# Copies, joins and weight roundings of the block products, tied to the program's order on ScalarE and VectorE

## The chip, the core and the metric

The kernel runs on one core of a Trainium2 chip. A core has a matrix engine (TensorE, "PE" in the profile, with its weight loads as "PEld"), VectorE ("DVE"), ScalarE ("ACT"), GpSimd ("POOL") and a queue that issues transfers ("SP"). Each engine works through its own list of instructions in the order in which the list was written; engines wait for each other by semaphores. The metric is the device time of one execution in microseconds.

## The reference

One inference step of a two-layer network over 640 tokens (512 latent, 128 context). Layer 0 mixes tokens with a state-space scan, layer 1 with differential attention. After each mixer comes the same kind of feed-forward network, and that is where the change lies:

```python
def conv_ffn(h, up_w, conv_w, conv_b, down_w):
    u = dwconv(h @ up_w, conv_w, conv_b)
    a, v = jnp.split(u, 2, axis=-1)
    return (jax.nn.silu(a) * v) @ down_w
```

Here `h` is 640 x 1024, `up_w` is 1024 x 5632, the convolution runs over three neighbouring tokens, and `down_w` is 2816 x 1024.

## The kernel before

Everything is kept transposed: 128 channels lie on the 128 partitions, the 640 tokens along the free axis. Every dense product is made of three matmuls: each operand is split into a rounded high part and the remainder, and high x high, high x low and low x high are added. For the weights the split is done on the chip. `cast` (L257) takes a loaded weight tile `raw` of 128 x 1024, rounds it on ScalarE into `whi` and subtracts on VectorE to get `wlo`; both go through `split_w` (L268). `nextw` (L277) hands out the next weight unit and has the one a few places further on cast; in the part of interest that is three units ahead (`AHEAD`). There are five buffers for cast units.

The 2816 hidden channels are 22 "pairs" of 128 (one half for `a`, one for `v`). The first `STD` of them (16 in layer 0, 5 in layer 1) are computed directly. The others, 6 in layer 0 and 17 in layer 1, are computed by the class `Blocks` (L46): a pair costs seven half-size products instead of eight, at the price of sums of the results. A product (L113) is 12 matmuls of 128 x 320. In `pair` (L138) product 1 goes into the PSUM area `a`, ScalarE copies it into the first half of `ua`; product 2 goes into `b` and VectorE adds ("joins") it to that; product 6 accumulates on `a`, and ScalarE copies again; product 5 goes into `c`; product 7 accumulates on `a`, ScalarE copies it into `uv` and VectorE joins `c`. Two products of a pair are finished inside the next pair: `third` (L159, product 3 on `c`, a join) and `fourth` (L164, product 4 on `a`, a copy), after which `epilogue` follows: a convolution of `ua` and one of `uv` (each one ScalarE instruction and four on VectorE), SiLU on ScalarE, a multiplication on VectorE, and the split of the result into `mh` (ScalarE) and `ml` (VectorE).

The program's order of the seven products in a pair is therefore 1, 2, 3 (of the pair before), 6, 4 (of the pair before, with its epilogue), 5, 7. Each weight unit serves two consecutive products, so a unit is cast at every other one.

The three areas lie in PSUM tiles of two halves each, columns 0 to 511 and 512 to 1023, three tiles in rotation (`banks`, L129). In every second pair ("even" below, the first of a stage among them) `a` and `b` are the halves of one tile, `ba` in the trace, and `c` is the first half of the next, `bb`. In the pair after it ("odd") `a` is the second half of that `bb`, and `b` and `c` are the halves of `bc`. The pairs run in stages with the down-projection (`po`) between them: 6 pairs in layer 0, then 3, 7 and 7 in layer 1. The two late products of a stage's last pair run after the first down-projection tile (`between`).

What sets the order: the program is written as one sequence, and a scheduler at compile time places each engine's instructions in an order of its own, as early as buffers and data allow by its estimate. Only an instruction passed through `tc.keep_in_program_order` is tied: it must stand behind the instruction that was written before it for the same engine. The helpers `act`, `tt`, `stt` and `mm` (L218 to L231) do this only while `fixed` is set, which is so in the kernel's first microseconds and not in the feed-forward networks. All ScalarE instructions of the helper show as line L222 in the profile, VectorE's as L225 and L228, the matmuls as L231; the tile names tell them apart.

## Time and profile before

| what | us |
|---|---|
| median of three runs (1838.42 to 1843.67) | 1839.06 |
| the profiled execution | 1841.66 |
| its span, first to last instruction | 1839.9 |
| first and last stretch with block products: layer 0 | 899 to 981 |
| layer 1, three stages | 1451 to 1496, 1540 to 1635, 1679 to 1775 |

The mean granted clock of TensorE was 0.995. Times inside the execution are counted from the span's start. In the chain that ended last, a piece such as "PE ba x12" is a run of twelve matmuls into that tile. A matmul's own duration in the trace overlaps its neighbours', so the length of a run is read from such pieces: twelve matmuls without a gap take 1.76.

### The profile page before, as it was taken

The numbers are of one execution on the slowest core, as the hardware profiler recorded it, in microseconds if no ns is written. First come the engines' busy times: TensorE is split into PE (matmuls) and PEld (weight loads), VectorE is DVE, ScalarE is ACT, GpSimd is POOL, SyncE is SP. The second block draws the span as 40 slices with busy tenths as digits, with TensorE's granted clock in tenths as the row PEclk, the third lists the DMA queues.
The fourth block names the chain that finished last, engine by engine and source line by source line (L and its number), as shares of the span: only waits on it lengthen the run. The fifth ranks groups of instructions, "written<-read, shape, count | busy, mean of one in ns | idle before, by whom it ended". The sixth has DMA issues, their size and how long they took to land.

```text
span 1839.9 us, 32867 instructions
## 1 busy us (share of the span) xinstructions
PE 1805.4 (98%) x12929; PEld 1711.4 (93%) x12929; DVE 1477.1 (80%) x2847; ACT 1022.3 (56%) x1904; POOL 55.6 (3%) x84
## 2 busy tenths in 40 slices
PE   7999999999999999999999999999999999999997
PEld 5799899989989999999999989999899999999997
DVE  5689999999848999998686788888879864774874
ACT  3379686879526442244354577777646543643651
POOL 0000000000001000001000000000001011100000
PEclk9999999999999999999999999999999999999998
DMA  9835244336556976667743212111047368863421
GB/s 346 272 109 142 96 123 138 115 134 171 165 179 194 268 239 197 213 206 202 221 134 103 70 54 70 62 49 57 23 144 180 97 184 229 257 173 104 138 87 58
DMA packets 108675, 276.05 MB, mean 150 GB/s; under 512 B 12284, under 2 KB 19048, under 8 KB 102504
## 3 DMA queue, kind: packets, MB, share of 16 engines
q1 hardware_dynamic: 100520, 225.19, 38.0%
q0 software_dynamic: 7424, 48.24, 11.2%
q8 instruction: 101, 1.65, 0.4%
q10 hardware_dynamic: 576, 0.52, 0.1%
q14 instruction: 54, 0.44, 0.1%
HBM read 267.95 MB, written 54.19 MB: 175 GB/s over the span
## 4 chain that ended last, share of the span: by engine, by line
PE 90%; DVE 4%; ACT 3%; DMA 2%; issue 1%; SPq 0%; DVEq 0%; ACTq 0%
PE po L231 25%; PE up L231 14%; PE bb L231 7%; PE ba L231 6%; PE bc L231 6%; PE z L231 6%; PE x L231 5%; PE st L231 5%; PE yp L231 3%; PE q L231 2%; PE ov L231 2%; PE sl L231 2%; PE k L231 1%; PE in L231 1%; PE v L231 1%; PE modrow L231 1%
## 5 line engine op out<-in xcount | busy, mean ns | idle before, releaser
L222 ACT ACTIVATE whi<-raw 128x1024 fp32r<-128x1024 f32 (+4 forms) x266 | 270.8, 1020 | 311.8 <-PE po L231 181.4
L228 DVE TENSOR_TENSOR wlo<-raw,whi 128x1024 fp32r<-128x1024 f32 (+4 forms) x266 | 312.2, 1174 | 74.2 <-ACT whi L222 69.2
L225 DVE SCALAR_TENSOR_TENSOR xr<-po,mod,xr 128x256 f32<-128x256 f32 (+2 forms) x231 | 89.1, 432 | 117.8 <-PE po L231 117.7
L231 PE MATMUL po<-ml,whi 128*128 128x256 f32 (+1 forms) x704 | 168.1, 310 | 0.0
L231 PE MATMUL po<-mh,wlo 128*128 128x256 f32 (+1 forms) x704 | 167.7, 309 | 0.0
L231 PE MATMUL po<-mh,whi 128*128 128x256 f32 (+1 forms) x704 | 167.7, 310 | 0.0
L231 PEld LDWEIGHTS po<-mh,whi 128*128 128x128 f32 x704 | 128.1, 188 | 0.8 <-ACT mh L222 0.5
L231 PEld LDWEIGHTS po<-ml,whi 128*128 128x128 f32 x704 | 128.6, 188 | 0.1
L231 PEld LDWEIGHTS po<-mh,wlo 128*128 128x128 f32 x704 | 128.7, 188 | 0.0
L231 PE MATMUL up<-h01h,wlo 128*128 128x256 f32 x464 | 105.7, 308 | 0.0
L231 PE MATMUL up<-h01h,whi 128*128 128x256 f32 x464 | 105.7, 308 | 0.0
L231 PE MATMUL up<-h01l,whi 128*128 128x256 f32 x464 | 105.6, 308 | 0.0
L231 PEld LDWEIGHTS up<-h01h,whi 128*128 128x128 f32 x464 | 84.4, 188 | 0.0
L231 PEld LDWEIGHTS up<-h01l,whi 128*128 128x128 f32 x464 | 84.4, 188 | 0.0
L231 PEld LDWEIGHTS up<-h01h,wlo 128*128 128x128 f32 x464 | 84.4, 188 | 0.0
L222 ACT ACTIVATE mh<-cv 128x640 fp32r<-128x640 f32 x44 | 32.4, 737 | 88.8 <-DVE cv L228 88.8
L689 DVE CUSTOM_DVE_ANT_0 junk<-mw,cbc 128x1024 bf16<-128x1024 f32 x48 | 58.5, 1219 | 9.5 <-DMA mw<-in_modT 9.4
L222 ACT ACTIVATE ca<-ca 128x640 f32<-128x640 f32 x44 | 32.3, 735 | 55.7 <-DVE ca L225 55.6
L231 PE MATMUL z<-h00h,whi 128*128 128x256 f32 (+1 forms) x256 | 63.0, 325 | 0.0
L231 PE MATMUL bb<-T,whi 128*128 128x320 f32 x264 | 61.6, 312 | 0.0
L222 ACT ACTIVATE e<-rb,Ctok 128x128 f32<-128x128 f32 x160 | 56.3, 389 | 8.5 <-issue 6.1
L222 ACT ACTIVATE e<-sl,sm 128x640 f32<-128x640 f32 x64 | 50.4, 792 | 18.2 <-DVE sm L1225 17.7
(579 smaller groups left out, 5316.4 us busy)
## 6 DMA issues: line engine op xcount, KB each, us to landing
wsum<-in_w_blk POOLq DMA_DIRECT2D x42, 768.0 KB, 7.2
raw<-in_w_blk SPq DMA_DIRECT2D x55, 512.0 KB, 4.1
mw<-in_modT SPq DMA_DIRECT2D x48, 512.0 KB, 4.1
raw<-wsum SPq DMA_DIRECT2D x92, 256.0 KB, 2.9
raw<-in_w_in SPq DMA_DIRECT2D x40, 512.0 KB, 5.1
rb<-rowd SPq DMA_DIRECT2D x40, 512.0 KB, 5.4
raw<-in_w_dn SPq DMA_DIRECT2D x32, 448.0 KB, 3.5
raw<-in_w_qkv SPq DMA_DIRECT2D x24, 512.0 KB, 3.4
```

The source lines that it names most:

```text
L222: return self.pin(self.nc.scalar.activation(out, in_, func, **k))
L225: return self.pin(self.nc.vector.scalar_tensor_tensor(out, in0, s, in1, op0, op1))
L228: return self.pin(self.nc.vector.tensor_tensor(out, a, b, op))
L231: return self.pin(self.nc.tensor.matmul(out, lhsT, rhs, start=start, stop=stop, **k))
L689: nc.vector.tensor_tensor_reduce(w if c else junk, w, cb[:, c, :], 1.0, 0.0, ALU.mult, ALU.add, self.mod[l][:, t, c:c + 1])
```

## The change

Two helpers are added, `evac` (a copy on ScalarE) and `join` (an addition or subtraction on VectorE), both always tied to the program's order. The copies and joins of `pair`, `third` and `fourth` use them. While a stage's pairs are running (`blocks` is set), `cast` uses them too, for `whi` and `wlo`. The instructions themselves, their operands and their number stay as they are; the epilogue and the matmuls are not tied.

```diff
     def pair(self, p):
...
         self.product(a, 1, p)
-        st.act(ua[:, c1], a, AF.Copy)
+        st.evac(ua[:, c1], a)
         self.product(b, 2, p)
-        st.tt(ua[:, c1], ua[:, c1], b, ALU.add)
+        st.join(ua[:, c1], ua[:, c1], b)
         if self.pend:
             self.third()
         self.product(a, 6, p)
-        st.act(ua[:, c2], a, AF.Copy)
+        st.evac(ua[:, c2], a)
         if self.pend:
             self.fourth()
         self.product(c, 5, p)
         self.product(a, 7, p)
-        st.act(uv[:, c2], a, AF.Copy)
-        st.tt(uv[:, c2], uv[:, c2], c, ALU.add)
+        st.evac(uv[:, c2], a)
+        st.join(uv[:, c2], uv[:, c2], c)
...
     def third(self):
...
-        self.st.tt(ua[:, HT:], ua[:, HT:], c, ALU.add)
+        self.st.join(ua[:, HT:], ua[:, HT:], c)
...
     def fourth(self):
...
-        self.st.act(uv[:, :HT], a, AF.Copy)
+        self.st.evac(uv[:, :HT], a)
         self.epilogue(p, ua, uv)
...
     def cast(self, upto):
...
-            self.split_w(hi, lo, r)
+            if self.blocks:
+                self.evac(hi, r)
+                self.join(lo, r, hi.bitcast(F32), ALU.subtract)
+            else:
+                self.split_w(hi, lo, r)
...
+    def evac(self, out, in_):
+        self.tc.keep_in_program_order(self.nc.scalar.activation(out, in_, AF.Copy))
+    def join(self, out, a, b, op=ALU.add):
+        self.tc.keep_in_program_order(self.nc.vector.tensor_tensor(out, a, b, op))
...
-                if done >= std:
+                self.blocks = done >= std
+                if self.blocks:
                     blk.pair(done)
...
-            self.down = True
+            self.down, self.blocks = True, False
```

## The prediction

> **What bounds the kernel now.** First the page's busy shares and its chain of waits, over the whole span.

> ```profile
> span 1839.9 us, 32867 instructions
> PE 1805.4 (98%) x12929; PEld 1711.4 (93%) x12929; DVE 1477.1 (80%) x2847; ACT 1022.3 (56%) x1904; POOL 55.6 (3%) x84
> PE 90%; DVE 4%; ACT 3%; DMA 2%; issue 1%; SPq 0%; DVEq 0%; ACTq 0%
> ```

> TensorE is the bound: 98% busy and 90% of the chain. A change of order on ScalarE and VectorE can therefore win only what TensorE now idles, and loses whatever it makes TensorE idle. Next, the busy time by stretches in the longest block stage (us of the stretch, then busy us of each engine, the granted clock).

> ```profile
> 1539.00:1635.00 96.00, 95.41 (x635) 92.83 (x634) 71.97 (x113) 54.38 (x78) 11.80 (x16) 1.00 0.85 240
> ```

> 95.4 of 96 us PE, 72 DVE, 54 ACT: the helpers have room in sum, but DVE is at 75%, so what counts is when each result arrives. Where PE does idle is seen in the chain that ended last, in order of time (start, length, what). Here is the worst place of that stage, and the rows of its like in the other three.

> ```profile
> 1602.43 1.75 PE bb L231 x11
> 1604.18 0.02 issue
> 1604.20 0.02 ACT whi L222
> 1604.23 0.86 issue
> ...
> 1605.17 0.43 ACT ua L222
> ...
> 1605.64 2.03 PE bb L231 x12
> ...
> 963.33 0.94 issue
> ...
> 1462.01 0.45 ACT uv L222
> ...
> 1465.03 0.94 issue
> ...
> 1743.59 0.86 issue
> ```

> A rounding `whi` of about 1 us slipped onto ScalarE just ahead of the copy `ua` on which the next product waited: 1605.64 - 1604.18 is 1.46 us lost. The four places of this kind (963, 1465, 1604, 1743) make 5.8, and a late copy at 1462 makes 0.5: **6.3 us** in all are what a better order can win outright. Besides these, runs of 12 matmuls show 1.88 to 2.03 instead of 1.76 where a product follows a copy or join directly; that is the turn-around of a semaphore, and I credit the order with none of it.

> **The change, part by part.** It adds and removes no instruction and no transfer; it moves ScalarE and VectorE instructions. I call the copies ua1 (after product 1), ua2 (after 6), uv2 (after 7) and uv1 (after product 4), the joins likewise. Behind whom does each now stand? `whi` of products 1, 2, 3, 6 and 4 stands between copies, at the start of a product and not at its end: that removes the stalls above, **-6.3**. But products 5 and 7 are written after the epilogue of the pair before. One of them casts a unit, so that `whi` is tied behind `mh`, and uv2 behind that `whi`. On VectorE `wlo` is tied behind `ml`, and the join of uv2 behind that `wlo`. Today's order is another (ScalarE, then VectorE, even pair around 1570; the `uv<-bb` copy is the uv1 of the odd pair before):

> ```profile
> 1570.32 0.41 ACT L222 ACTIVATE ua<-ba 128x320 f32<-128x320 f32 x1
> 1571.58 0.42 ACT L222 ACTIVATE uv<-bb 128x320 f32<-128x320 f32 x1
> 1572.03 0.92 ACT L222 ACTIVATE cv<-uv,fcw 128x640 f32<-128x640 f32 x1
> 1573.49 1.05 ACT L222 ACTIVATE whi<-raw 128x1024 fp32r<-128x1024 f32 x1
> 1574.51 0.44 ACT L222 ACTIVATE uv<-ba 128x320 f32<-128x320 f32 x1
> 1576.52 0.74 ACT L222 ACTIVATE mh<-cv 128x640 fp32r<-128x640 f32 x1 [1.57 <-DVE cv L228]
> ```

> ```profile
> 1573.43 1.93 DVE L225 SCALAR_TENSOR_TENSOR cv<-uv,fcw,cv 128x511 f32<-128x511 f32 x4
> 1575.28 0.48 DVE L228 TENSOR_TENSOR uv<-uv,bb 128x320 f32<-128x320 f32 x1
> 1575.67 0.81 DVE L228 TENSOR_TENSOR cv<-ca,cv 128x640 f32<-128x640 f32 x1
> 1576.41 1.21 DVE L228 TENSOR_TENSOR wlo<-raw,whi 128x1024 fp32r<-128x1024 f32 x1
> 1577.55 0.81 DVE L228 TENSOR_TENSOR ml<-cv,mh 128x640 fp32r<-128x640 f32 x1
> ```

> Today uv2 (1574.51) is 2.0 us ahead of `mh`, and its join (1575.28) 2.3 ahead of `ml`. Tied, from the start of uv1: to the convolution 0.45 (1572.03 - 1571.58), the convolution 0.92 and its four taps 1.93, the multiplication 0.81, `mh` 0.74, `whi` 1.02 (1574.51 - 1573.49). Sum: uv2 begins at **+5.9**, ends at +6.3; after `whi` come `wlo` 1.21 and the join 0.48: the join ends at **+7.6**. (The other convolution, of `ua`, isn't tied and needs only product 3, so I take it as done before.) Today uv2 begins at 1574.51 - 1571.58 = 2.9.

> Who waits for uv2 and its join? TensorE:

> ```profile
> 1572.71 1.76 PE ba L231 x12
> 1574.47 1.47 PE bc L231 x10
> 1575.94 1.89 PE bb L231 x12
> ...
> 1542.10 0.19 PEld L231 LDWEIGHTS ba<-h11h,whi 128*128 128x128 f32 x1 [0.20 <-ACT ua L222]
> ...
> 1544.78 0.30 PEld L231 LDWEIGHTS ba<-T,whi 128*128 128x128 f32 x2 [0.18 <-DVE ua L228]
> ```

> `ba` at 1572.71 is product 7, `bc` the next pair's product 2, `bb` the next pair's product 1: it starts 0.2 after the join of uv2 (1575.28 + 0.48 = 1575.76), because it shares the tile `bb` with the `c` which that join reads. The two load rows show the same rule elsewhere: product 2 at 1542.10 waits for the copy of product 1, which lies in the other half of `ba`, and product 6 at 1544.78 for the join that reads product 2 there. So copies and joins of a tile block both halves, and I use that throughout.

> *Odd pair to even pair.* Time 0 is uv1's start, tied behind ua2, that is 0.45 after product 6's end. Products 5 and 7 run to 2 x 1.76 - 0.45 = 3.1, product 1 of the new pair to 4.8. Product 2 then needs ua1, which stands behind uv2 (6.3) and this product's own `whi` (1.0), and ends at 7.6; product 3 needs the join, 7.6; product 4 needs uv2, and its weights are those whose `whi` ended at 5.9 and `wlo` at 7.1. TensorE idles from 4.8 to 7.1: **2.3 us**.

> *Even to odd.* Here a `whi` stands between ua2 and uv1, so that uv1 starts about when product 5 does; 5, 7 and the next product 2 run to 5.2, product 4 starts after uv2 at 6.4: **1.2**. It covers until the join at 7.6; product 1 runs 7.7 to 9.4, its copy ends at 9.9, the rest of product 4 and product 3 end at 11.8. Product 5 or 6 needs the join of ua1, now tied behind product 2's `wlo`: 9.9 + 1.0 + 1.2 + 0.5 = 12.6. **0.9** more, so 2.1; the 0.9 alone after a stage's first pair, which has no epilogue before it.

> Count by stages of 6, 3, 7 and 7 pairs: odd to even 2 + 1 + 3 + 3 = 9 times 2.3 = 20.7; even to odd with an epilogue 2 + 0 + 2 + 2 = 6 times 2.1 = 12.6; four first pairs at 0.9 = 3.6. Together **+36.9**. Some of the turn-arounds of 0.1 to 0.2 us fall into these stalls: about two in each of the 19, say **-4** (an estimate from the 1.88 to 2.03 above). `whi` coming about a unit (two products, 3.5 us) later than today costs nothing, covered by a lead of three units, 10.5 us. The epilogue itself ends no later. Sum: 36.9 - 6.3 - 4 = **+26.6**.

> No run shows TensorE's own order after the change, which the scheduler makes anew. Its bounds: -6.3, if the fillers cover every wait; and without any filler (no early product 2 or 4) odd to even 7.7 - 4.8 = 2.9 and even to odd 7.7 - 3.45 + 0.9 = 5.1 each, 9 x 2.9 + 6 x 5.1 + 3.6 = 60, less 10.3: +50. I take +26.6, with the fillers that the order of today shows (`bc` ahead of `bb` at 1574.47).

> **The forecast.** 1841.66 of the profiled execution + 26.6 = 1868.3; that execution is 2.6 over the median of the runs, so 1865.7 on their scale. About 0.3% (5.5 us) is what a measurement of this kernel can tell from no change.

> **Rivals.**
> *Faster: the order frees the copies.* If TensorE always has a product whose inputs are ready while uv2 waits, only the -6.3 stays: 1832.8 on the median's scale. For it: the four stalls are real, and each is a `whi` ahead of a copy. Against: it needs 4 us of other ready products after product 7, and the tiles leave one (product 2 or 1). It decides from the point where uv2's delay of 3.0 (5.9 - 2.9) is covered. 0.12.
> *No change: the halves are independent.* If a product waited only for what lies in its own half, products 1 and 2 of the new pair could both run before uv2 is copied, to 6.6; only the weights of product 4 would be missed, 0.5 us, nine times: 4.5 - 6.3 = -1.8, 1837.3. The row at 1542.10 and the start at 1575.94 speak against it. 0.13.
> [...]
> *Slower by twice as much: no filler.* +50, 1889. For it: the order on TensorE is fixed at compile time by estimates, and a filler that stands on the wrong side of a waiting product is no filler. Against: today's order shows the scheduler placing them well. 0.13.
> In this rival TensorE idles over 4 us at a time. [...]

> ```profile
> 1604.00:1606.00 2.00, 1.41 (x10) 1.15 (x9) 0.70 (x1) 1.71 (x3) 0.00 (x0) 1.00 1.08 256
> ```

> [...]
> *The forecast*, +10 to +40 us: 0.62.

> **How the numbers follow.** Faster 0.12, same 0.13, slower 0.62 + 0.13 = 0.75. The range reaches down over the rival of no change to 1835 and up over the one without fillers to 1892; it leaves out the faster one and a tail above, under 0.2 together.

> **What would show it.** In the changed trace: `mh` ahead of `uv` on ScalarE in every pair but a stage's first; idle before PE's products 1, 2 or 4 ended by ACT uv or DVE uv, 1 to 2.5 us each, about 15 times; no stall at a `whi` ahead of `ua` like that of 1604; the stretch of the 7-pair stage longer by about 10 us, everything outside the block stages unchanged. Wrong if uv2 leaves ScalarE ahead of `mh`, or if TensorE's idle time in the stages doesn't grow.

## The result and the profile after

The changed kernel takes 1890.68 us (median of 5 runs, 1884.81 to 1891.8) against 1839.87 (1838.42 to 1843.67): a ratio of **1.0266**, 95% interval 1.0255 to 1.0277, 50.8 us slower. The forecast said slower, 1865.7, range 1835 to 1892. The execution whose profile follows is the fastest of the five: 1884.81, with a span 43.0 us longer than before (1882.9 against 1839.9). Why the other four are longer still is answered below.

The page of the changed kernel: span, busy times, the shares of the chain that ended last. Then, by stretches, the first of the two 7-pair stages of layer 1 (us, then busy us of each engine, the granted clock).

```profile
span 1882.9 us, 32820 instructions
PE 1818.2 (97%) x12929; PEld 1717.7 (91%) x12929; DVE 1480.8 (79%) x2847; ACT 1021.5 (54%) x1904; POOL 55.6 (3%) x84
PE 83%; DVE 7%; ACT 7%; DMA 2%; issue 1%; SPq 0%; DVEq 0%; ACTq 0%
```

```profile
1553.80:1663.70 109.90, 97.96 (x632) 93.89 (x631) 74.37 (x114) 54.14 (x78) 11.80 (x16) 0.98 0.76 207
```

The same work as before, but the chain has moved: 7 points of it have gone from TensorE to VectorE and ScalarE. The stage that took 95.6 us (1539.82 to 1635.39 in the chain of before) takes 109.9, 14.3 more, and its clock shows 0.98 instead of 1.00. The 6-pair stage and the other 7-pair stage grew likewise; the 3-pair stage, with one place where the epilogue stands ahead of a waiting product, by under 1.

The order on ScalarE at the end of an odd pair (start, length, what), and then VectorE's rows of the same place:

```profile
1572.11 0.44 ACT L274 ACTIVATE ua<-bb 128x320 f32<-128x320 f32 x1 [1.24 <-PE bb L231]
1572.44 0.43 ACT L274 ACTIVATE uv<-ba 128x320 f32<-128x320 f32 x1
1572.91 0.93 ACT L222 ACTIVATE cv<-uv,fcw 128x640 f32<-128x640 f32 x1
1573.73 0.72 ACT L222 ACTIVATE ca<-ca 128x640 f32<-128x640 f32 x1
1576.77 0.74 ACT L222 ACTIVATE mh<-cv 128x640 fp32r<-128x640 f32 x1 [2.31 <-DVE cv L228]
1577.41 1.04 ACT L274 ACTIVATE whi<-raw 128x1024 fp32r<-128x1024 f32 x1
1578.36 0.42 ACT L274 ACTIVATE uv<-bb 128x320 f32<-128x320 f32 x1
```

```profile
1577.54 0.82 DVE L228 TENSOR_TENSOR ml<-cv,mh 128x640 fp32r<-128x640 f32 x1 [0.80 <-ACT mh L222]
1578.48 1.23 DVE L278 TENSOR_TENSOR wlo<-raw,whi 128x1024 fp32r<-128x1024 f32 x1
1579.63 0.48 DVE L278 TENSOR_TENSOR uv<-uv,bc 128x320 f32<-128x320 f32 x1
```

Line L274 is the new copy on ScalarE, L278 the new join on VectorE. (Some line numbers given for the kernel before are off: there `Blocks` begins at L52, `product` at L101, `banks` at L118, `pair` at L128, `third` at L149, `fourth` at L154, `cast` at L258.) The copy uv2 (`uv<-bb` at 1578.36) stands behind `mh` and `whi`, 5.92 us after uv1 (1572.44), and its join behind `ml` and `wlo`; it ends 7.67 after uv1 (1579.63 + 0.48). ScalarE sat 2.31 us waiting for `mh`'s input. Product 7, which uv2 copies, had ended at 1575.87; the copy stood behind `mh` and `whi` for another 2.5 us.

At the end of an even pair the path is longer. These are ScalarE's rows of uv1, the SiLU and uv2 there, 6.47 us from uv1 to uv2:

```profile
1588.61 0.43 ACT L274 ACTIVATE uv<-bb 128x320 f32<-128x320 f32 x1
1589.07 0.74 ACT L222 ACTIVATE ca<-ca 128x640 f32<-128x640 f32 x1
...
1595.08 0.42 ACT L274 ACTIVATE uv<-ba 128x320 f32<-128x320 f32 x1
```

Who waited for it: the waits of TensorE in the changed kernel (who, for whom; us in all, times, longest), then the only two of before in the same products.

```profile
PE bb L231 <- ACT uv L274: 15.3, 9, 2.1
PE ba L231 <- ACT uv L274: 11.8, 6, 2.0
...
PE bc L231 <- DVE ua L278: 3.2, 6, 0.6
PE bb L231 <- DVE wlo L278: 2.3, 6, 0.4
...
PE bb L231 <- ACT ua L274: 1.4, 6, 0.2
...
PE ba L231 <- ACT ua L274: 0.9, 3, 0.3
```

```profile
PE bb L231 <- ACT ua L222: 1.8, 4, 0.6
...
PE ba L231 <- ACT uv L222: 0.5, 1, 0.5
```

Nine waits on `bb` (odd to even) and six on `ba` (even to odd) end with uv: 27.1 us. With the smaller ones 34.9, against 2.3 before: **+32.6 of the 43.0**. Some of the rest is a lower clock. Here is TensorE after the wait at 1578.83, and the same microseconds by stretches:

```profile
1577.32 0.31 PE L231 MATMUL ba<-h11h,wlo 128*128 128x320 f32 x1
1578.83 0.56 PE L231 MATMUL bb<-T,whi 128*128 128x320 f32 x2 [1.20 <-ACT uv L274]
1579.76 0.42 PE L231 MATMUL bb<-T,wlo 128*128 128x320 f32 x1 [0.38 <-DVE wlo L278]
...
1581.12 0.47 PE L231 MATMUL ba<-h11l,whi 128*128 128x320 f32 x1
1581.39 0.47 PE L231 MATMUL ba<-h11h,wlo 128*128 128x320 f32 x1
```

```profile
1577.00:1578.00 1.00, 0.63 (x5) 0.37 (x3) 0.46 (x1) 1.00 (x2) 0.00 (x0) 1.00 0.77 156
1578.00:1579.00 1.00, 0.17 (x1) 0.17 (x2) 0.88 (x2) 1.00 (x3) 0.00 (x0) 1.00 0.12 25
1579.00:1580.00 1.00, 0.62 (x3) 0.36 (x4) 1.00 (x2) 1.00 (x3) 0.10 (x1) 1.00 0.00 0
1580.00:1581.00 1.00, 1.00 (x7) 1.00 (x7) 1.00 (x2) 0.99 (x2) 1.00 (x2) 0.80 0.36 39
1581.00:1582.00 1.00, 1.00 (x6) 1.00 (x5) 0.24 (x1) 0.00 (x0) 0.60 (x2) 0.50 1.08 354
...
1583.00:1584.00 1.00, 1.00 (x5) 1.00 (x5) 0.43 (x2) 0.00 (x0) 0.00 (x0) 0.50 0.94 385
1584.00:1585.00 1.00, 1.00 (x8) 1.00 (x8) 1.00 (x2) 0.00 (x0) 0.00 (x0) 0.99 1.08 404
```

First a wait of 1.20 for uv2, then one of 0.38 for `wlo`, and then the clock (the column after POOL) falls: 0.80 in the stretch from 1580, 0.50 in the three from 1581, 0.99 in the one from 1584. Counted as time at 0.50, the 1.7 us that these five lack of full clock are some 3.4 us, from 1580.6 on. Matmuls start 0.27 apart there (1581.12 to 1581.39) instead of 0.147 (1.76 / 12). In stretches of 1 us the block stages of this execution show four such falls, and those of before none. Each fall loses 1.7 us, half of its 3.4: **+6.8**. (The mean clocks of the whole executions give 1882.9 x 0.008 = 15.1 here and 1839.9 x 0.005 = 9.2 before, so +5.9; they are rounded to a thousandth, which is 1.9 us.) What is left of 43.0, 3.6 us, I put down to the turn-around at the new waits: the lines above and the two of before count 36 waits against 5, so it is about 0.1 for each new one. No run separates it. In the four other runs the clock was 0.988 to 0.990: 1888.8 x 0.012 = 22.7 in the median one, 7.6 more than in the profiled one, and its time is 5.9 longer.

### The profile page after: what moved, and what is told of

Read it like the earlier page. It is cut to its first block, busy times and chain, and to the rows that moved or that the text cites. A ratio compares the mean times of both kernels' runs of the same rounds, so it can differ in the third digit from the quotient of the medians.

```text
span 1882.9 us, 32820 instructions
## 1 busy us (share of the span) xinstructions
PE 1818.2 (97%) x12929; PEld 1717.7 (91%) x12929; DVE 1480.8 (79%) x2847; ACT 1021.5 (54%) x1904; POOL 55.6 (3%) x84
## 4 chain that ended last, share of the span: by engine, by line
PE 83%; DVE 7%; ACT 7%; DMA 2%; issue 1%; SPq 0%; DVEq 0%; ACTq 0%
PE po L231 24%; PE up L231 13%; PE z L231 6%; PE x L231 5%; PE ba L231 5%; PE bc L231 5%; PE st L231 5%; PE bb L231 4%; PE yp L231 3%; PE q L231 2%; PE ov L231 2%; DVE cv L225 2%; ACT whi L274 2%; PE sl L231 1%; PE k L231 1%
## 5 line engine op out<-in xcount | busy, mean ns | idle before, releaser
L222 ACT ACTIVATE whi<-raw 128x1024 fp32r<-128x1024 f32 (+4 forms) x187 | 189.4, 1015 | 218.1 <-PE po L231 163.6
L228 DVE TENSOR_TENSOR wlo<-raw,whi 128x1024 fp32r<-128x1024 f32 (+4 forms) x187 | 218.4, 1168 | 37.8 <-ACT whi L222 32.8
L225 DVE SCALAR_TENSOR_TENSOR xr<-po,mod,xr 128x256 f32<-128x256 f32 (+2 forms) x231 | 89.2, 433 | 119.6 <-PE po L231 119.5
L231 PE MATMUL po<-ml,whi 128*128 128x256 f32 (+1 forms) x704 | 168.6, 310 | 0.3 <-DVE ml L228 0.3
L231 PE MATMUL po<-mh,whi 128*128 128x256 f32 (+1 forms) x704 | 168.2, 311 | 0.0
L231 PE MATMUL po<-mh,wlo 128*128 128x256 f32 (+1 forms) x704 | 167.9, 310 | 0.0
L278 DVE TENSOR_TENSOR wlo<-raw,whi 128x1024 fp32r<-128x1024 f32 (+1 forms) x79 | 93.9, 1190 | 48.3 <-ACT whi L274 46.4
L231 PEld LDWEIGHTS po<-ml,whi 128*128 128x128 f32 x704 | 128.6, 188 | 0.9 <-DVE ml L228 0.7
L231 PEld LDWEIGHTS po<-mh,whi 128*128 128x128 f32 x704 | 128.2, 188 | 0.9 <-ACT mh L222 0.5
L231 PEld LDWEIGHTS po<-mh,wlo 128*128 128x128 f32 x704 | 128.8, 188 | 0.0
L231 PE MATMUL up<-h01h,wlo 128*128 128x256 f32 x464 | 105.6, 308 | 0.0
L231 PE MATMUL up<-h01l,whi 128*128 128x256 f32 x464 | 105.6, 308 | 0.0
L231 PE MATMUL up<-h01h,whi 128*128 128x256 f32 x464 | 105.6, 308 | 0.0
L222 ACT ACTIVATE mh<-cv 128x640 fp32r<-128x640 f32 x44 | 32.5, 738 | 116.4 <-DVE cv L228 116.4
L274 ACT ACTIVATE whi<-raw 128x1024 fp32r<-128x1024 f32 (+1 forms) x79 | 79.9, 1025 | 15.4 <-PE po L231 15.4
L231 PEld LDWEIGHTS up<-h01h,wlo 128*128 128x128 f32 x464 | 84.4, 188 | 0.0
L231 PEld LDWEIGHTS up<-h01l,whi 128*128 128x128 f32 x464 | 84.4, 188 | 0.0
L231 PEld LDWEIGHTS up<-h01h,whi 128*128 128x128 f32 x464 | 84.4, 188 | 0.0
L231 PE MATMUL bb<-T,whi 128*128 128x320 f32 x264 | 60.6, 312 | 15.3 <-ACT uv L274 15.3
L231 PE MATMUL z<-h00h,whi 128*128 128x256 f32 (+1 forms) x256 | 62.9, 325 | 0.0
L222 ACT ACTIVATE e<-rb,Ctok 128x128 f32<-128x128 f32 x160 | 56.3, 389 | 8.5 <-issue 6.1
```

The costliest lines, as they stand in the source:

```text
L222: return self.pin(self.nc.scalar.activation(out, in_, func, **k))
L225: return self.pin(self.nc.vector.scalar_tensor_tensor(out, in0, s, in1, op0, op1))
L228: return self.pin(self.nc.vector.tensor_tensor(out, a, b, op))
L231: return self.pin(self.nc.tensor.matmul(out, lhsT, rhs, start=start, stop=stop, **k))
L274: self.tc.keep_in_program_order(self.nc.scalar.activation(out, in_, AF.Copy))
L278: self.tc.keep_in_program_order(self.nc.vector.tensor_tensor(out, a, b, op))
```

## The experiments

The theory: uv2 is late because it is tied behind a `whi` that is tied behind `mh`; TensorE idles for it at 15 places, and after four of those its clock falls to 0.50. In the cuts of the diffs below, `...` stands for lines left out. The rivals named in the expectations:
- A: the order of the other copies costs (uv1 no longer ahead of ua2).
- B: VectorE's order is the cause.
- C: the roundings come too late.
- D: ties cost wherever the epilogue stands.
- E to G belong to one run each.

All diffs are against the changed kernel. Each ratio is to the kernel before, measured on the same chip.

| run | median us | ratio (95% interval) | median clock |
|---|---|---|---|
| e1, roundings free | 1843.22 | 1.0014 (1.0005 to 1.0023) | 0.996 |
| e2, only roundings tied | 1838.61 | 0.9992 (0.9983 to 1.0002) | 0.996 |
| e3, only ScalarE tied | 1891.63 | 1.0287 (1.0269 to 1.0306) | 0.988 |
| e4, only VectorE tied | 1860.35 | 1.0111 (1.0096 to 1.0126) | 0.995 |
| e5, epilogue later | 1846.3 | 1.0033 (1.0022 to 1.0045) | 0.996 |
| e6, rounding ahead of the epilogue | 1883.24 | 1.0229 (1.0214 to 1.0244) | 0.990 |
| e7, rounding twice | 1919.46 | 1.043 (1.0414 to 1.0445) | 0.981 |
| e8, only `whi` and uv2 tied | 1880.17 | 1.0214 (1.0199 to 1.0229) | 0.991 |
| e9, all but uv2 and its join tied | 1842.5 | 1.0009 (1.0 to 1.0018) | 0.997 |
| e10, filler matmuls | 1882.41 | 1.0222 (1.0206 to 1.0237) | 0.994 |
| e11, e2 again, more runs | 1838.85 | 0.9987 (0.9979 to 0.9996) | 0.997 |

**e1: the roundings free.**

```diff
-            if self.blocks:
+            if False:
                 self.evac(hi, r)
```

> The copies and joins stay tied, the weight roundings (whi, wlo) are free again. Theory (uv2 is late because it stands behind a whi that stands behind mh): the whi that uv2 is tied to may now go ahead of mh, so uv2 follows product 7 at once; 1835 to 1846 us, no idle before a product that ends with ACT uv over 1 us. Rival A (the order of the copies themselves costs: uv1 no longer ahead of ua2): 1850 to 1865, with idle before products that wait for uv1's slot. Rival B (VectorE's order, joins behind wlo and ml): wlo is free too, so like the theory.

1843.22, 3.0 us over the kernel before on that chip: as the theory says, and rival A (1850 to 1865) falls.

**e2: only the roundings tied.** `evac` and `join` tie only in `cast`.

```diff
-                self.evac(hi, r)
-                self.join(lo, r, hi.bitcast(F32), ALU.subtract)
+                self.evac(hi, r, tied=True)
+                self.join(lo, r, hi.bitcast(F32), ALU.subtract, tied=True)
```

> Only the weight roundings are tied, the copies and joins are free. Theory: whi still stands behind mh, but uv2 may pass both; the roundings have a lead of three units, 10.5 us, and cover it: 1835 to 1846. Rival C (the roundings themselves come too late for their products): near 1890, with PE waiting for whi or wlo instead of uv. Rival A: like before.

1838.61: rival C falls, and the lead of the roundings covers their later place. So neither half of the change costs much alone. By the theory the loss needs both ties, `whi` to `mh` and uv2 to `whi`; e8 tests these two alone.

**e3 and e4: one engine at a time.**

```diff
 # e3, join
-        self.tc.keep_in_program_order(self.nc.vector.tensor_tensor(out, a, b, op))
+        self.nc.vector.tensor_tensor(out, a, b, op)
 # e4, evac
-        self.tc.keep_in_program_order(self.nc.scalar.activation(out, in_, AF.Copy))
+        self.nc.scalar.activation(out, in_, AF.Copy)
```

> ScalarE's copies and roundings are tied, VectorE's joins and remainders are free. Theory: the 15 idle times that end with ACT uv (1.3 to 2.1 us each in the changed kernel, 28 in sum) stay, the further 0.4 to 0.6 behind wlo and the join shrink; 1866 to 1884. Rival B (VectorE's order is the cause): back to 1838 to 1850.

> VectorE's joins and remainders are tied, ScalarE is free. Theory: uv2 is early again, but its join still stands behind ml and a wlo, so the even-to-odd places idle for it while the odd-to-even ones don't: 1845 to 1865. Rival B: near 1890.

The waits of TensorE in e3, then in e4:

```profile
PE bb L231 <- ACT uv L274: 17.4, 9, 2.4
PE ba L231 <- ACT uv L274: 11.8, 6, 2.0
...
PE bb L231 <- DVE wlo L278: 2.2, 6, 0.4
```

```profile
PE bb L231 <- ACT uv L274: 8.7, 8, 1.9
PE ba L231 <- ACT uv L274: 4.2, 8, 0.7
...
PE bb L231 <- DVE uv L278: 1.2, 1, 1.2
```

Rival B falls: with ScalarE alone the whole loss is there, 9 and 6 waits as before. The time is above what was expected (1866 to 1884), since untying VectorE did not shrink the waits for `wlo`, which follows its `whi` anyway, and since the clock fell further (0.987 in the profiled execution, against 0.992). VectorE alone costs 20 us, within the range; but the reason given was wrong in part, as its waits end with the copy uv on ScalarE and not with the join. uv2 was not early in e4, as had been expected. At the three longest of those waits, 1.95 us each, ScalarE shows `whi`, `mh` and then uv2 (1596.76, 1597.72 and 1598.35 at one of them): the scheduler chose this order itself, with nothing tied on ScalarE. Why it did so with VectorE tied is not shown. So a late uv2 can come about without the two ties as well.

**e5: the epilogue written behind uv2 and its join**, all ties kept.

```diff
-        if self.pend:
-            self.fourth()
+        done = self.fourth() if self.pend else None
         self.product(c, 5, p)
...
         st.join(uv[:, c2], uv[:, c2], c)
+        if done:
+            self.epilogue(*done)
...
     def fourth(self):
...
-        self.epilogue(p, ua, uv)
         self.pend = None
+        return p, ua, uv
...
-            self.fourth()
+            self.epilogue(*self.fourth())
```

> All ties as in the change, but the epilogue of the pair before is written behind uv2 and its join instead of ahead of product 5. Theory (only the place of the epilogue in the program's order makes the ties costly): uv2 is ahead of mh again, the next pair's ua1 now stands behind mh, which is ready by about the time that product 1 ends, and product 4 fills what is left; 1836 to 1850. Rival D (ties cost by taking freedom, wherever the epilogue stands): over 1865.

1846.3: 44 us of the loss are gone with every tie in place, so rival D falls. What the ties cost here is decided by what the program writes ahead of them. Six microseconds remain; TensorE's waits in e5 show eleven short ones for joins, 5.9 us in all, that the kernel before has not:

```profile
PE bc L232 <- DVE ua L279: 3.2, 6, 0.6
PE ba L232 <- DVE ua L279: 2.7, 5, 0.6
```

**e6: the unit of product 5 or 7 rounded ahead of the epilogue.**

```diff
         self.st.evac(uv[:, :HT], a)
+        if self.st.blocks:
+            self.st.cast(self.st.wi + AHEAD)
         self.epilogue(p, ua, uv)
```

> All ties as in the change, but the weight unit of product 5 or 7 is rounded ahead of the epilogue, so that uv2 stands directly behind mh. Theory: uv2 is about 1.0 us earlier at each of 15 places and the join another 1.2; the idle before products that wait for uv2 halves from 28 to about 13, the 0.6 behind wlo go: 20 to 27 us less than the change, and the clock stays up: 1858 to 1872. Rival E (the time is lost by the roundings being late, not by uv2 standing behind mh): back to 1840.

A miss: 7.4 us less than the change instead of 20 to 27. ScalarE's rows of e6 show why:

```profile
1568.28 0.43 ACT L276 ACTIVATE uv<-ba 128x320 f32<-128x320 f32 x1
1568.60 1.06 ACT L276 ACTIVATE whi<-raw 128x1024 fp32r<-128x1024 f32 x1
1569.55 0.92 ACT L224 ACTIVATE cv<-uv,fcw 128x640 f32<-128x640 f32 x1
...
1573.73 0.74 ACT L224 ACTIVATE mh<-cv 128x640 fp32r<-128x640 f32 x1 [2.63 <-DVE cv L230]
1574.37 0.42 ACT L276 ACTIVATE uv<-bb 128x320 f32<-128x320 f32 x1
```

The `whi` has only moved within the same chain: now it runs between uv1 and the convolution that leads to `mh`. From uv1 to uv2 it is 1574.37 - 1568.28 = 6.09, no less than 5.92. TensorE's waits for uv sum to 29.0 us against 27.1; those for `wlo` are gone, and with the ones for joins all make 31.4 against 34.9. Rival E (1840) falls as well.

**e7: the `whi` between `mh` and uv2 computed twice.**

```diff
         self.epilogue(p, ua, uv)
+        self.st.again = self.st.blocks
...
                 self.evac(hi, r)
+                if self.again:
+                    self.evac(hi, r)
+                    self.again = False
```

> As the change, but the whi that stands between mh and uv2 is computed twice (1.0 us more of ScalarE at 19 places, 15 of them ahead of a waiting product). Theory: each of the 15 places idles 1.0 us longer, and the clock falls more often: 15 to 30 us more than the change, 1905 to 1922. Rival F (ScalarE's delay is covered and something else sets the time): within 5 us of the change, 1886 to 1896.

```profile
PE bb L232 <- ACT uv L278: 25.5, 10, 3.2
PE ba L232 <- ACT uv L278: 18.3, 6, 3.1
```

28.8 us more than the change. The waits for uv grew from 27.1 to 43.8: about 1.08 more at each of the 15 places, which is the added rounding, and one new wait of 0.44. The clock fell to 0.981. Rival F falls.

**e8 and e9: two ties, and all but two.**

```diff
 # e8: whi and this copy tied, all others free
-        st.evac(uv[:, c2], a)
+        st.evac(uv[:, c2], a, tied=True)
...
-                self.evac(hi, r)
+                self.evac(hi, r, tied=True)
...
 # e9: this copy and its join free, all others tied
-        st.evac(uv[:, c2], a)
-        st.join(uv[:, c2], uv[:, c2], c)
+        st.act(uv[:, c2], a, AF.Copy)
+        st.tt(uv[:, c2], uv[:, c2], c, ALU.add)
```

> Only whi and the copy uv2 are tied; ua1, ua2, uv1, the joins and wlo are free. Theory: this alone puts uv2 behind mh and whi, so nearly the whole loss is there: 1872 to 1894. Rival A (the other copies' order carries a good part of it): 1845 to 1868.

> All ties as in the change except those of the copy uv2 and its join, which are free. Theory: uv2 leaves ScalarE ahead of mh again and its join ahead of ml; the 28 us of idle that end with ACT uv are gone, 1836 to 1850. Rival D (the ties as a whole cost by the freedom they take): over 1860.

```profile
1576.77 0.44 ACT L222 ACTIVATE uv<-ba 128x320 f32<-128x320 f32 x1
1579.01 0.74 ACT L222 ACTIVATE mh<-cv 128x640 fp32r<-128x640 f32 x1 [1.80 <-DVE cv L228]
1579.66 1.04 ACT L274 ACTIVATE whi<-raw 128x1024 fp32r<-128x1024 f32 x1
```

Those are ScalarE's rows in e9: uv2 is ahead of `mh` again. The two ties of e8 bring 40.0 of the 50.8 us; leaving uv2 and its join out (e9) takes all but about 1 away. That is the cause of these 40, shown from both sides. The other 11 come with the remaining ties: in e8 TensorE's waits at these products make 27.4 us against 34.9 (none for a join of ua, and 11.0 instead of 15.3 for uv on `bb`), and the clock is 0.991 against 0.988. Which of the remaining ties brings them was not tried.

**e10: 8 matmuls more after product 7**, 19 times; their result is not used.

```diff
             self.fourth()
+            late = True
+        else:
+            late = False
...
+        if late:
+            x = self.t["11", 0][0]
+            d = st.bank("m", "dum")
+            for i in range(8):
+                st.mm(d[:, :HT], x[:, :P], x, i == 0, i == 7)
```

> As the change, with 8 matmuls of 128x320 more after product 7 in the 19 pairs that have an epilogue ahead of it; their result is not used. 8 x 0.147 is 1.2 us each, 22 us of TensorE work in all. Theory (part of the loss is a lower granted clock after the idle times, 0.988 to 0.992 against 0.995 to 0.998 before): where the matmuls fall into an idle time they are free and hold the clock up, so the clock is 0.994 or more; the time is 1880 to 1895 in spite of 22 us more work. Rival G (the clock has nothing to do with the idle times): the clock stays at 0.988 to 0.992 and the time is 1890 to 1912.

More work, less time: 1882.41, 8.3 us under the changed kernel, and a clock of 0.994 against 0.988 to 0.992. The scheduler did not put all of them into idle time; waits for uv of 9.8 us remain of 27.1. Nor did it spread them evenly, and that makes a comparison inside one execution (the first 7-pair stage, then the last 73 us of the second):

```profile
1553.00:1665.00 112.00, 111.58 (x736) 107.73 (x735) 77.98 (x121) 56.96 (x82) 11.47 (x16) 1.00 0.76 208
1744.00:1817.00 73.00, 63.75 (x390) 61.39 (x391) 47.52 (x73) 35.30 (x51) 0.00 (x0) 0.93 0.38 119
```

In the first stretch 80 of the 152 added matmuls ran; TensorE has no wait for uv there, and the clock stays at 1.00. In the second none ran; three waits of 2.0 to 2.1 us remain, and the clock falls behind each of them. Rival G falls: the lower clock follows the idle time, and filling part of that raises it.

**e11: e2 once more.**

> The kernel with only the weight roundings tied, once more with more rounds, since it was the only one at or under the time before (0.9992, interval 0.9983 to 1.0002). If its gain is real, 1837 to 1839.5 and an interval under 1; if not, the interval holds 1. Both stay far under the 2.8 us that TensorE idled for copies before plus its turn-arounds.

0.9987 (0.9979 to 0.9996): a gain of about 0.1%, the only version under the time before, and barely.

## Why the prediction was right in kind and short in size

*The path of uv2.* Right to a tenth for the odd-to-even places, for which it was worked out: uv2 forecast at +5.9 after uv1 and its join's end at +7.6; the rows show 5.92 and 7.67. At the even-to-odd places it is 6.47 instead of 5.9: the SiLU (0.74) runs between uv1 and the convolution there, and the sum had no term for it.

*Who waits, and how often.* Right: 9 odd-to-even and 6 even-to-odd places were counted, and the waits view has `bb` 9 and `ba` 6 times. The sizes fit less well. Odd to even was put at 20.7 in all; measured 15.3 for uv, 2.3 for `wlo` and 0.9 for ua on `ba`, together 18.5. Even to odd was put at 12.6, 2.1 each; measured 11.8 for uv, 3.2 for the join of ua and 1.4 for ua on `bb`, together 16.4 or 2.7 each. The 3.6 after the stages' first pairs does not appear. That 36.9 was forecast and 34.9 measured is in part luck: these misses offset each other.

*The credit of 6.3.* This step failed. It took the stretch that the chain spends on ScalarE (1604.18 to 1605.64) for idle time of TensorE. The chain follows what came last; TensorE meanwhile ran matmuls of another product. The prediction's own row of 1604 to 1606 shows it busy for 1.41 of 2.00 us, so not 1.46 but 0.59 was idle there. TensorE's own waits of before there are 1.8 + 0.5 = 2.3, so no more than that was to be won.

*The credit of 4 for turn-arounds* is not borne out: what is left of the sum is +3.6 and not -4. I put it down to turn-arounds that the new waits brought instead of hiding; no run separates it.

*The clock.* The sum had no term for it. That idle stretches of the length in the sum, up to 2.3 us, leave the clock up was assumed; the row of 1604 to 1606 shows it (1.00) for 0.59 us of idle time only. What the clock lost is +6.8 in the profiled execution, and by the mean clocks about 7.6 more in the median run, an estimate to some 2 us. So: 34.9 - 2.3 + 3.6 + 6.8 = 43.0 instead of 26.6, and about 8 more of clock for the median.
From 1577 to 1581 TensorE was busy 2.42 of 4 us, its longest wait there was 1.20, and the clock fell to 0.50.

*The rivals.* The one without fillers gave 1889, closest to the median, but by the wrong way: it needs 5.1 us of idle at each even-to-odd place, and 2.7 were measured. The early products 2 and 4 ran as forecast; its number was met by the clock. The measured +50.8 lies outside the +10 to +40 that the forecast called its own, and 1.3 us inside a range whose upper end was set by this rival; that it lies inside is luck. The faster one fell: uv2's delay of 3.0 was not covered. The one with independent halves fell by its time; whether a product would have to wait for the other half of its tile was not tried by itself. Of the signs named, the order on ScalarE and the 15 waits came as forecast; the 7-pair stage grew by 14.3 us instead of about 10.

## What to carry to other kernels

A tie to the program's order costs what the program happens to have written ahead of it: before an instruction is tied, list the instruction that stands before it on its engine and what that one waits for. Here one short copy stood behind the end of a long chain over two engines, and moving one call (e5) or freeing that copy and its join (e9) removed nearly all of the loss. And read idle time of the bounding engine from its own waits, not from the chain of waits, which counts a late engine's time even while the bound one has other work.

## What the runs showed of the hardware

| wait ends | its length | first 1-us stretch below full clock | mean clock of that stretch and the next ones |
|---|---|---|---|
| 923.81 | 1.19 | 925 | 0.63, 0.50, 0.50, 0.67 |
| 971.68 | 1.97 | 973 | 0.52, 0.50, 0.50, 0.77 |
| 1578.83 | 1.20 | 1580 | 0.80, 0.50, 0.50, 0.50, 0.99 |
| 1732.54 | 1.18 | 1734 | 0.60, 0.50, 0.50, 0.69 |

Each time 1.7 us of full clock are missing, which makes 3.4 us at half. Three of these four waits are among the shortest, 1.2 us with one of 0.4 close behind. The stretch behind a wait of 2.09 that ends at 1611.53 keeps its clock (stretch, busy time of PE, clock):

```profile
1611.00:1618.00 7.00, 6.09 (x40) 1.00 0.95 245
```

So the length of a wait alone does not decide. What else does is not shown by any run.

The block stages of the kernel before and of e1, e2, e5 and e9 show no such fall, and TensorE's longest wait for a copy, join or rounding of the block products is 0.7 there; e4 shows 1, e10 3, the change 4, e6 and e8 8 each, e3 12, and e7, with waits up to 3.2 us, 17. Runs of one kernel can differ in the same way: 1884.81 us at a clock of 0.992, 1890.15 to 1891.8 at 0.988 to 0.990, though only one execution of each kernel was traced. And 22 us of useless matmuls made the changed kernel 8.3 us faster (e10).
